# A two-layer transformer on one core: another opening with filler matmuls, and a landing price for transfers issued by ScalarE

## The chip, the core and the metric

The kernel runs on one core of one Trainium2 chip. The metric is the device time of one execution in microseconds; less is better. The engines are called PE (TensorE, the matmuls; PEld its weight loads), DVE (VectorE), ACT (ScalarE), POOL (GpSimd) and SP (SyncE, which here only issues transfers).

## The reference, cut to what matters

Two layers work on x of 256 tokens by 1024 channels, in float32. Each layer is a SwiGLU network, a mixer, and a second SwiGLU network, each behind a norm that is modulated by the condition c:

```python
c_act = jax.nn.silu(c)
for layer in range(2):
    mod = (c_act @ ada_w[layer] + ada_b[layer]).reshape(B, 3, 3, D_MODEL)
    h = modulate(x, norm_g[layer, 0], mod[:, 0, 0], mod[:, 0, 1])     # rmsnorm(x)*g*(1+scale)+shift
    x = x + 0.5 * mod[:, 0, 2][:, None, :] * swiglu(h, ffn_w13[layer, 0], ffn_w2[layer, 0])
    h = modulate(x, norm_g[layer, 1], mod[:, 1, 0], mod[:, 1, 1])
    y = swa_mixer(...) if layer == 0 else fox_mixer(...)
    x = x + mod[:, 1, 2][:, None, :] * y
    h = modulate(x, norm_g[layer, 2], mod[:, 2, 0], mod[:, 2, 1])
    x = x + 0.5 * mod[:, 2, 2][:, None, :] * swiglu(h, ffn_w13[layer, 1], ffn_w2[layer, 1])
# fox_mixer: log_f = log_sigmoid(fl + b_f); F = cumsum(log_f); s = q.k + F[q] - F[k], causal softmax, @ v
```

swa_mixer is attention in a window of 128 with a sink and a relative bias; both mixers have 16 query heads of 64 channels, and q and k are normed per head. The inner width of the SwiGLU networks is 2816. ada_w, the modulation's weights, is 1024 by 9216 in each layer.

## The kernel before

**Matmuls.** Every float32 product is three matmuls (`mm3`). `split` has ACT cast a landed weight piece `wraw` (128x1024, 512 KB) to `whi`, and DVE subtract to get the rest `wlo`; the activations are split in the same way into a high and a low part of hT. The three are whi by hT high, whi by hT low, and wlo by hT high. In the trace and in the order below all of them read `pa<-whi,hT` or `ps<-wlo,hT`; pa and ps are both PSUM banks.

**Order.** The whole program is first recorded, with every instruction on a named engine (or, through `rec.also`, on one of two). `Recorder.run` then plays a list scheduler over it: it gives each instruction a duration, works out due times from PE's order, and on each engine picks the ready instruction with the earliest due time; `rec.urgent` sets a due time by hand. A transfer's end is taken from its bytes at 400 GB/s behind the transfers before it, with 2000 ns more for those that POOL issues. The order in which the plan starts them is the order in which each engine's queue holds them on the chip, so an instruction whose input is late holds up all that stand behind it. Weights are issued by SP, at most 8 in flight. Since one helper emits everything, all instructions stand on one line (L238) in the profile, and tiles tell them apart.

**Opening.** SP loads c into one row of `gate`, then x in two halves, then the weights. ACT issues two small transfers (`colb`, the modulation's bias by column, and `gcol`, the norm gains); POOL issues `qkg` (gains of q and k), `sink` and `bfb` (the forget bias) through its software queue. ACT takes Silu of c (1x1024), two matmuls with `ones` broadcast it to 128 rows, and ACT copies it to `cb`. `rstd` squares x on ACT (t, ss, u, rs), `norm` scales it to `xn`, on DVE for the first half of the tokens and on ACT for the second. `start` transposes xn in 16 pieces into two tiles `xT`, of four k blocks each, and then runs the first 1024 of the inner columns in 8 k steps. A k step loads two pieces of ada, on which DVE makes two dot products with cb (`SCALAR_TENSOR_TENSOR wraw,mod<-wraw,cb`, written into `mod`), and two pieces of weight (`w13s`), and issues h, hT high (ACT), hT low (DVE) and 24 matmuls of 128x512.

**First FFN after that.** The other columns follow with `sil` (silu times up), its transposes (`ps<-ident,sil`) and `gT`, the high and low part of the transposed product, beside which DVE works off the rest of layer 0's modulation, paced by a table.

**Second mixer.** For groups of heads PE makes q and k, ACT squares them (`sq`), DVE sums (`qss`), POOL takes the power (`qrs`), DVE scales (`qn`), and PE transposes (`pa<-ident,qn`). `fox_maps` makes the running sums of log f, writes them to DRAM (`foxsc`) and reads them back to all partitions in four transfers of 512 KB, on ACT's queue, as `M`; DVE adds F and the mask (`M<-M,F,cmask`) before the softmax uses it (`t,nm<-ps,M`).

Of the kernel before, what the change touches and what calls it, by code (L numbers as in the profile page):

```python
# [44 lines left out]
TABLE = 1283.0  # L45
TC = {}
# [119 lines left out]
class Op:  # L166
    __slots__ = ("eng", "emit", "dur", "deps", "succ", "bases", "due", "n", "wait", "ready", "start", "end",
                 "bytes", "at", "bg", "urgent", "alts", "paced", "port", "part", "group", "table")
# [10 lines left out]
class Recorder:  # L179
    def __init__(self):  # L180
        self.ops, self.bases, self.slots, self.pe, self.releases = [], [], {}, 0.0, []
        self.bg, self.urgent, self.paced, self.marks, self.group = False, None, None, [], None

    def add(self, eng, real, method, a, k):
# [11 lines left out]
        o.table = None  # L196
# [95 lines left out]
    def run(self, window=None):  # L292
# [62 lines left out]
        pes = sorted((o for o in ops if o.eng == "PE"), key=lambda o: o.at)  # L355
        for o in ops:
            o.wait, o.ready = len(o.deps), 0.0
            if not o.wait:
                heapq.heappush(pending, (0.0, o.n))

        def finish(o, t, end):
# [12 lines left out]
            for s in o.succ:  # L374
                s.wait -= 1
                s.ready = max(s.ready, o.end + lat(o, s))
                if not s.wait:
                    heapq.heappush(pending, (s.ready, s.n))
                    heapq.heappush(events, s.ready)

        while len(done) < len(ops):
# [11 lines left out]
            for e in engines:  # L393
                while busy[e] <= t:
# [3 lines left out]
                    for i, (due, n) in enumerate(avail[e][:60]):  # L398
# [10 lines left out]
                        if fits(o):  # L409
# [13 lines left out]
                            break  # L423
                    if pick is None:
                        break
# [55 lines left out]
def _build(ctx, rec, tc, nc, ap, out):  # L481
# [23 lines left out]
    crow = gate[0:1]  # L505
    rec.urgent = -60e3
# [21 lines left out]
    ones = cp.tile([P, P], F32, name="ones")  # L528
    G.memset(ones, 1.0)
# [10 lines left out]
    qkg = cp.tile([P, 2, 2], F32, name="qkg")  # L540
    sink = cp.tile([P, NH], F32, name="sink")
    msink = cp.tile([P, NH], F32, name="msink")
    bfb = cp.tile([P, NH], F32, name="bfb")
# [134 lines left out]
    def norm(h, eng=None):  # L678
        rs = rstd(h)
        xn = []  # L680
        for dh in range(2):
            c = slice(dh * 512, dh * 512 + 512)
            t = bp.tile([P, 512], F32, tag="b", name="xn")
            if eng is A:
                A.activation(t, x[h][:, c], AF.Copy, scale=rs)
            else:
                V.tensor_scalar(out=t, in0=x[h][:, c], scalar1=rs, scalar2=None, op0=ALU.mult)
# [24 lines left out]
    def start(hT):  # L712

        xn = [norm(0), norm(1, A)]
        xT = []
        for g in range(2):
            t = wp.tile([P, 4, S], F32, tag="w", name="xT")
            for h in range(2):
                pt = psum()
                for j in range(4):  # L720
                    T.transpose(pt[:, j * P : j * P + P], xn[h][g][:, j * P : j * P + P], ident)
                A.copy(t[:, :, h * P : h * P + P], pt.rearrange("p (a b) -> p a b", a=4))
            xT.append(t)
        banks = [[pool_() for _ in range(2)] for pool_ in (pacc, pacc, psum, psum)]
        mod = new_mod()

        def modulated(k):
            for m in range(2):
# [3 lines left out]
            o = V.tensor_scalar(out=t, in0=xT[k // 4][:, k % 4, :], scalar1=mod[1][:, k : k + 1],  # L732
                                scalar2=mod[0][:, k : k + 1], op0=ALU.mult, op1=ALU.add)
            rec.also(o, A, "activation", t, xT[k // 4][:, k % 4, :], AF.Identity, scale=mod[1][:, k : k + 1],
                     bias=mod[0][:, k : k + 1])
# [5 lines left out]
        for k in range(KT):  # L741
# [3 lines left out]
            for c in range(NST):  # L745
                a = (c % 2) * 512
# [458 lines left out]
def _layout(inputs):  # L1205
# [28 lines left out]
    a["qkg"] = np.stack([np.stack([col(f["swa_q_g"][0]), col(f["swa_k_g"][0])], 1),  # L1234
                         np.stack([col(f["fox_q_g"][0]), col(f["fox_k_g"][0])], 1)], 1)
    a["sink"] = f["swa_sink"].reshape(1, NH)
    a["bf"] = f["fox_b_f"].reshape(1, NH)
# [28 lines left out]
```

## Time and profile before

| | |
|---|---|
| median of 3 runs | 995.08 us (993.34 to 995.79) |
| the profiled execution's own time | 994.5 us |
| its span in the trace | 992.7 us |
| granted TensorE clock, mean | 1.00 |
| busy: PE, DVE, ACT, POOL | 972.6, 776.9, 528.2, 48.2 us |
| moved by DMA | 252.73 MB, 255 GB/s over the span |

Times in the rows are microseconds from the span's start; a row of the timeline is the start, the busy time, the engine, the operation with output and inputs, a count, and in brackets the idle time before it with what ended it. A row of the waits is what waited, for what, and then the total, the number of times and the longest.

### The profile page before, as it was taken

What the parts mean: (1) busy time and instruction counts of PE and PEld (TensorE: products, weight loads), DVE (VectorE), ACT (ScalarE), POOL (GpSimd) and SP (SyncE); (2) the same over time, 40 slices, a digit from 0 to 9 for tenths busy, and PEclk for the clock granted to TensorE, in tenths of its full rate; (3) what the DMA queues carried; (4) which work ended last, traced back from release to release, by engine and by line L of the source; (5) the groups of instructions that cost most, each with busy time, mean ns of one, the idle gap of its engine ahead of it and who ended that gap; (6) DMA issues with size and microseconds to landing.
All of it is one profiled execution on the core that took longest, in us unless ns stands there. A gap on an engine that the chain in (4) does not pass through costs nothing.

```text
span 992.7 us, 13662 instructions
## 1 busy us (share of the span) xinstructions
PE 972.6 (98%) x4766; PEld 816.3 (82%) x4766; DVE 776.9 (78%) x1396; ACT 528.2 (53%) x946; POOL 48.2 (5%) x73
## 2 busy tenths in 40 slices
PE   6999999999999999999999999999999999999998
PEld 4878788798888888888888888889899888888886
DVE  5999989985899988767898788658788998554622
ACT  6583434465986454444554453437677776444420
POOL 1000000012100000000100000001221010000000
PEclk9999999999999999999999999999999999999999
DMA  9999999856347987776788879744437458656501
GB/s 338 409 390 383 402 361 409 307 172 215 129 156 252 337 334 285 291 294 233 275 317 304 312 279 352 247 157 161 139 112 266 161 197 282 224 198 220 211 8 64
DMA packets 74247, 252.73 MB, mean 255 GB/s; under 512 B 8497, under 2 KB 11969, under 8 KB 74178
## 3 DMA queue, kind: packets, MB, share of 16 engines
q1 hardware_dynamic: 73186, 249.63, 68.6%
q10 hardware_dynamic: 896, 2.21, 0.6%
q8 instruction: 37, 0.61, 0.2%
q0 software_dynamic: 96, 0.02, 0.2%
q14 instruction: 32, 0.26, 0.1%
HBM read 249.95 MB, written 1.88 MB: 254 GB/s over the span
## 4 chain that ended last, share of the span: by engine, by line
PE 91%; DVE 4%; ACT 2%; DMA 2%; issue 1%; POOL 0%; SPq 0%; DVEq 0%; POOLq 0%
PE ps L238 57%; PE pa L238 34%; DVE wraw L238 1%; DVE wlo L238 1%; DMA wraw<-in_w13s 1%; DMA M<-foxsc 1%; ACT t L238 1%; POOL qrs L238 0%; ACT PT L238 0%; DVE t L238 0%; DVE gT L238 0%; DVE sil L238 0%; ACT whi L238 0%; SPq L238 0%; DVE qss L238 0%
## 5 line engine op out<-in xcount | busy, mean ns | idle before, releaser
L238 PE MATMUL ps<-whi,hT 128*128 128x512 f32 (+2 forms) x1728 | 534.8, 382 | 0.0
L238 ACT CAST whi<-wraw 128x1024 fp32r<-128x1024 f32 (+2 forms) x328 | 329.5, 1024 | 218.6 <-DMA wraw<-in_w 72.4
L238 DVE TENSOR_TENSOR wlo<-wraw,whi 128x1024 fp32r<-128x1024 f32 (+2 forms) x328 | 381.3, 1180 | 67.0 <-ACT whi L238 49.2
L238 PEld LDWEIGHTS ps<-whi,hT 128*128 128x128 f32 x1728 | 321.5, 188 | 52.9 <-issue 0.6
L238 PE MATMUL ps<-wlo,hT 128*128 128x512 f32 (+2 forms) x864 | 328.1, 381 | 0.0
L238 PE MATMUL pa<-whi,gT 128*128 128x512 f32 x704 | 218.0, 391 | 0.0
L238 DVE SCALAR_TENSOR_TENSOR wraw<-wraw,cb 128x1024 f32<-128x1024 f32 x144 | 173.3, 1218 | 15.5 <-DMA wraw<-in_ada 15.1
L238 PEld LDWEIGHTS ps<-wlo,hT 128*128 128x128 f32 x864 | 162.4, 188 | 26.1 <-issue 0.2
L238 PEld LDWEIGHTS pa<-whi,gT 128*128 128x128 f32 x704 | 131.9, 188 | 27.2
L238 PE MATMUL pa<-wlo,gT 128*128 128x512 f32 x352 | 133.3, 390 | 0.0
L238 ACT ACTIVATE sil<-ps 128x256 f32<-128x256 f32 x84 | 32.0, 384 | 105.6 <-PE ps L238 105.4
L238 PEld LDWEIGHTS pa<-wlo,gT 128*128 128x128 f32 x352 | 66.1, 188 | 13.6
L238 DVE TENSOR_TENSOR sil<-sil,ps 128x256 f32<-128x256 f32 x84 | 34.6, 414 | 48.2 <-ACT sil L238 48.1
L238 DVE TENSOR_TENSOR gT<-ps,gT 128x256 fp32r<-128x256 f32 x88 | 33.5, 415 | 8.9 <-ACT gT L238 8.9
L238 PE MATMUL pa<-whi,OT 128*128 128x512 f32 x128 | 39.1, 393 | 0.0
L238 PE MATMUL pa<-PT,zeroed 128*128 128x256 f32 (+1 forms) x192 | 36.3, 287 | 0.5 <-DVE PT L238 0.4
L238 ACT ACTIVATE t<-x 128x512 f32<-128x512 f32 x24 | 15.0, 625 | 40.8 <-DVE x L238 38.9
L238 DVE SCALAR_TENSOR_TENSOR t<-gate,pa 128x512 f32<-128x512 f32 (+1 forms) x26 | 15.6, 640 | 25.6 <-DMA gate<-gsc 12.9
L238 ACT CAST gT<-ps 128x256 fp32r<-128x256 f32 x88 | 29.1, 378 | 12.2 <-PE ps L238 11.6
L238 PEld LDWEIGHTS pa<-PT,zeroed 128*128 128x128 f32 x192 | 30.1, 191 | 3.8 <-DVE PT L238 1.2
L238 POOL TENSOR_TENSOR qrs<-qss,mhalf 128x4 f32<-128x4 f32 (+1 forms) x24 | 26.8, 1118 | 87.3 <-DVE qss L238 86.3
L238 PE MATMUL ps<-ident,sil 128*128 128x128 f32 x176 | 27.9, 272 | 2.6 <-DVE sil L238 1.4
(113 smaller groups left out, 650.7 us busy)
## 6 DMA issues: line engine op xcount, KB each, us to landing
wraw<-in_ada SPq DMA_DIRECT2D x144, 512.0 KB, 7.5
wraw<-in_w13b SPq DMA_DIRECT2D x132, 512.0 KB, 6.3
wraw<-in_w SPq DMA_DIRECT2D x88, 512.0 KB, 5.6
wraw<-in_w13a SPq DMA_DIRECT2D x28, 512.0 KB, 10.2
wraw<-in_fwin SPq DMA_DIRECT2D x28, 384.0 KB, 3.8
wraw<-in_w13s SPq DMA_DIRECT2D x16, 512.0 KB, 10.2
wraw<-in_swin SPq DMA_DIRECT2D x16, 384.0 KB, 5.2
wraw<-in_swout SPq DMA_DIRECT2D x8, 512.0 KB, 3.7
```

The lines of the kernel that those rows point to most:

```text
L238: return lambda: getattr(real, method)(*[un(v) for v in a], **{n: un(v) for n, v in k.items()})
```

## The change

Two parts are made together. The opening: 21 filler matmuls of 128x512 on a tile of zeros (`wz`), which the scheduler issues on PE whenever nothing else is ready; the five small inputs in one transfer `small` on ACT's queue, none on POOL's; an early Silu of one column; the Silu of c in the evacuation of the broadcast; the squares of x on either of ACT and DVE; xn on DVE alone, piece by piece; the second half of the transposes inside k step 0; h always on ACT. And the plan's costs: a transfer over 100 KB that ACT issues lands 2400 ns later in the plan, which moves the order in the second mixer (`small` counts too).

```diff
+NWARM = 21
 # Recorder.run, the choice of the next instruction:
+                    if pick is None and e == "PE" and fillers and fillers[0].wait == 0 and t >= fillers[0].ready:
+                        o = fillers.pop(0)
+                        busy[e] = t + o.dur * (2 if cold else 1)
+                        active += busy[e] - t
+                        ...
+                        continue
 # Recorder.run, the cost of a DMA:
-                        o.end = dma + 2000 * (e == "POOL")
+                        o.end = dma + (2000 if e == "POOL" else 2400 if e == "ACT" and o.bytes > 1e5 else 0)
 # _build:
+    warm = psum()
+    wz = wp.tile([P, 512], F32R, tag="w", name="wz")
+    G.memset(wz.bitcast(F32), 0.0)
+    rec.filler = True
+    for _ in range(NWARM):
+        T.matmul(warm, wz[:, 0:P], wz, start=True, stop=True)
+    rec.filler = False
+    rec.urgent = -70e3
+    tb = cp.tile([P, 1], F32, name="tb")
+    A.activation(tb, ones[:, 0:1], AF.Silu)
...
-    colb = cp.tile([P, 2, 9, KT], F32, name="colb")
-    A.dma_start(colb, ap["colb"])
+    small = cp.tile([P, 232], F32, name="small")
+    A.dma_start(small, ap["small"])
+    colb = small[:, 0:144].rearrange("p (l s k) -> p l s k", l=2, s=9)
+    gcol = small[:, 144:192].rearrange("p (s k) -> p s k", s=6)
+    qkg = small[:, 192:196].rearrange("p (a b) -> p a b", a=2)
+    sink = small[:, 196:212]
+    bfb = small[:, 212:228]
-    gcol = cp.tile([P, 6, KT], F32, name="gcol")
-    A.dma_start(gcol, ap["gcol"])
...
-    A.activation(crow, crow, AF.Silu)
     for i in range(2):
         T.matmul(pc, ones[0:1, :], crow[:, i * 512 : i * 512 + 512], start=True, stop=True)
-        A.copy(cb[:, i * 512 : i * 512 + 512], pc)
+        A.activation(cb[:, i * 512 : i * 512 + 512], pc, AF.Silu)
...
-        G.dma_start(qkg, ap["qkg"])
-        G.dma_start(sink, ap["sink"].to_broadcast([P, NH]))
-        G.dma_start(bfb, ap["bf"].to_broadcast([P, NH]))
...
-    def rstd(h):
+    def rstd(h, first=False):
-            A.activation(t, x[h][:, c], AF.Square, scale=1.0 / 32.0, accum_out=ss[:, dh : dh + 1])
+            o = A.activation(t, x[h][:, c], AF.Square, scale=1.0 / 32.0, accum_out=ss[:, dh : dh + 1])
+            if first:
+                rec.also(o, V, "scalar_tensor_tensor", out=t, in0=x[h][:, c], scalar=1.0 / 1024.0, in1=x[h][:, c],
+                         op0=ALU.mult, op1=ALU.mult, accum_out=ss[:, dh : dh + 1])
...
     def start(hT):
-        xn = [norm(0), norm(1, A)]
+        rs = [rstd(h, True) for h in range(2)]
-        for g in range(2):
+        def transposed_x(g):
             for h in range(2):
+                xn = bp.tile([P, 512], F32, tag="b", name="xn")
+                V.tensor_scalar(out=xn, in0=x[h][:, g * 512 : g * 512 + 512], scalar1=rs[h], ...)
                 for j in range(4):
-                    T.transpose(pt[:, j * P : j * P + P], xn[h][g][:, j * P : j * P + P], ident)
+                    T.transpose(pt[:, j * P : j * P + P], xn[:, j * P : j * P + P], ident)
+        transposed_x(0)
...
-            o = V.tensor_scalar(out=t, in0=xT[k // 4][:, k % 4, :], scalar1=mod[1][:, k : k + 1], ...)
-            rec.also(o, A, "activation", t, xT[k // 4][:, k % 4, :], AF.Identity, ...)
+            A.activation(t, xT[k // 4][:, k % 4, :], AF.Identity, scale=mod[1][:, k : k + 1], bias=mod[0][:, k : k + 1])
...
             for c in range(NST):
+                if k == 0 and c == 1:
+                    transposed_x(1)
```

Lines are now L240. Nearly nothing changes in SP's queue; POOL loses its three transfers.

PE, from its first matmul, before (hT_214 is the high part, hT_226 the low part):

```order
L238 MATMUL ps<-gate,ones 128x512 x2
L238 MATMUL ps<-ident,xn 128x128 x16
L238 MATMUL pa<-whi,hT_214 128x512
L238 MATMUL pa<-wlo,hT_214 128x512
L238 MATMUL pa<-whi,hT_214 128x512
L238 MATMUL pa<-wlo,hT_214 128x512
L238 MATMUL pa<-whi,hT_214 128x512
L238 MATMUL pa<-whi,hT_226 128x512 x2
L238 MATMUL pa<-wlo,hT_214 128x512
```

and with the change (hT_209 and hT_220):

```order
L240 MATMUL ps<-wz 128x512 x4
L240 MATMUL ps<-gate,ones 128x512 x2
L240 MATMUL ps<-wz 128x512 x9
L240 MATMUL ps<-ident,xn 128x128 x4
L240 MATMUL ps<-wz 128x512 x2
L240 MATMUL ps<-ident,xn 128x128 x4
L240 MATMUL ps<-wz 128x512 x6
L240 MATMUL pa<-whi,hT_209 128x512
L240 MATMUL pa<-wlo,hT_209 128x512
L240 MATMUL pa<-whi,hT_209 128x512
L240 MATMUL pa<-wlo,hT_209 128x512
L240 MATMUL pa<-whi,hT_220 128x512 x2
L240 MATMUL ps<-ident,xn 128x128 x8
```

The fillers stand around the broadcasts and the transposes, and 8 transposes have moved behind the sixth real matmul.

ACT, from its first instruction, before:

```order
L238 DMA colb<-in_colb 128x144
L238 DMA gcol<-in_gcol 128x48
L238 ACT_TABLE_LOAD
L238 ACTIVATE gate<-gate 1x1024
L238 ACTIVATE t,ss<-x_94 128x512
L238 ACTIVATE t,ss<-x_99 128x512 x2
L238 COPY cb<-ps 128x512
L238 ACTIVATE t,ss<-x_94 128x512
L238 ACTIVATE xn<-x_99,rs 128x512
L238 COPY cb<-ps 128x512
L238 CAST whi<-wraw 128x1024
L238 COPY xT<-ps 128x4x128 x2
```

and with the change:

```order
L240 DMA small<-in_small 128x232
L240 ACT_TABLE_LOAD
L240 ACTIVATE tb<-ones 128x1
L240 ACTIVATE t,ss<-x_90 128x512
L240 ACTIVATE cb<-ps 128x512 x2
L240 COPY xT<-ps 128x4x128
L240 CAST whi<-wraw 128x1024
L240 COPY xT<-ps 128x4x128
L240 ACTIVATE h_207<-xT,mod_192,mod_178 128x256
L240 CAST hT_209<-h_207 128x256
```

Behind the weight's cast ACT now has one evacuation of xT ahead of h, where before it had two and an xn and a second cast.

In the k steps from 2 on, the low part of hT stands in DVE's queue behind two wlo instead of one.

DVE before the first gT of the first FFN, before:

```order
L238 TENSOR_TENSOR wlo<-wraw,whi 128x1024
L238 TENSOR_TENSOR sil<-sil,ps 128x256 x4
L238 TENSOR_TENSOR wlo<-wraw,whi 128x1024 x6
L238 TENSOR_TENSOR gT<-ps,gT 128x2x128 x8
L238 TENSOR_TENSOR sil<-sil,ps 128x256
L238 SCALAR_TENSOR_TENSOR wraw,mod_772<-wraw,cb 128x1024
```

and with the change:

```order
L240 TENSOR_TENSOR wlo<-wraw,whi 128x1024
L240 TENSOR_TENSOR sil<-sil,ps 128x256 x4
L240 TENSOR_TENSOR wlo<-wraw,whi 128x1024 x5
L240 TENSOR_TENSOR gT<-ps,gT 128x2x128 x8
L240 TENSOR_TENSOR sil<-sil,ps 128x256
L240 TENSOR_TENSOR wlo<-wraw,whi 128x1024 x2
```

One wlo of six has moved behind the gT.

DVE in the second mixer, at the first tile M, before:

```order
L238 TENSOR_TENSOR qn<-ps,qrs 128x256
L238 TENSOR_TENSOR wlo<-wraw,whi 128x768
L238 SCALAR_TENSOR_TENSOR M_6799<-M_6799,F,cmask 128x256
L238 SCALAR_TENSOR_TENSOR M_6856<-M_6799,F,cmask 128x128
L238 TENSOR_REDUCE qss<-sq 128x4
L238 TENSOR_SCALAR qss<-qss 128x4
L238 SCALAR_TENSOR_TENSOR M_6799<-M_6799,F,cmask 128x256
L238 TENSOR_TENSOR zeroed<-ps,zeroed 128x2x64
L238 TENSOR_TENSOR qn<-ps,qrs 128x256
L238 SCALAR_TENSOR_TENSOR M_6856<-M_6799,F,cmask 128x128
L238 SCALAR_TENSOR_TENSOR M_6799<-M_6799,F,cmask 128x256
```

and with the change:

```order
L240 TENSOR_TENSOR qn<-ps,qrs 128x256
L240 TENSOR_TENSOR wlo<-wraw,whi 128x768
L240 TENSOR_REDUCE qss<-sq 128x4
L240 TENSOR_SCALAR qss<-qss 128x4
L240 TENSOR_TENSOR zeroed<-ps,zeroed 128x2x64
L240 TENSOR_TENSOR qn<-ps,qrs 128x256
L240 SCALAR_TENSOR_TENSOR M_6816<-M_6816,F,cmask 128x256
L240 SCALAR_TENSOR_TENSOR M_6908<-M_6816,F,cmask 128x128
```

qss and qn stand ahead of the work on M, where before two instructions on M stood ahead of qss and a third behind it.

More of the change, by code (lines that the diff above doesn't have):

```diff
@@ L167 @@
     __slots__ = ("eng", "emit", "dur", "deps", "succ", "bases", "due", "n", "wait", "ready", "start", "end",
-                 "bytes", "at", "bg", "urgent", "alts", "paced", "port", "part", "group", "table")
+                 "bytes", "at", "bg", "urgent", "alts", "paced", "port", "part", "group", "table", "filler")
 class Engine:
@@ L354, in run @@
         low, group, last, table = 0, None, None, None
-        pes = sorted((o for o in ops if o.eng == "PE"), key=lambda o: o.at)
+        pes = sorted((o for o in ops if o.eng == "PE" and not o.filler), key=lambda o: o.at)
+        fillers = [o for o in ops if o.filler]
         for o in ops:
             o.wait, o.ready = len(o.deps), 0.0
-            if not o.wait:
+            if not o.wait and not o.filler:
                 heapq.heappush(pending, (0.0, o.n))
@@ L376, in finish @@
                 s.ready = max(s.ready, o.end + lat(o, s))
-                if not s.wait:
+                if not s.wait and not s.filler:
                     heapq.heappush(pending, (s.ready, s.n))
@@ L505, in _build @@
     crow = gate[0:1]
+    ones = cp.tile([P, P], F32, name="ones")
+    G.memset(ones, 1.0)
+    warm = psum()
[8 more added lines that the diff above has]
+    A.activation(tb, ones[:, 0:1], AF.Silu)
     rec.urgent = -60e3
@@ L676, in rstd, with norm @@
         return rs
-    def norm(h, eng=None):
+    def norm(h):
         rs = rstd(h)
```

27 lines of the change are left out of this document (10 added, 17 removed).

## The prediction

> **What bounds the kernel now.** I read the page first: busy times, then the chain that ended last.
>
> ```profile
> PE 972.6 (98%) x4766; PEld 816.3 (82%) x4766; DVE 776.9 (78%) x1396; ACT 528.2 (53%) x946; POOL 48.2 (5%) x73
> PE 91%; DVE 4%; ACT 2%; DMA 2%; issue 1%; POOL 0%; SPq 0%; DVEq 0%; POOLq 0%
> ```
>
> PE (TensorE) is busy for 98% of the span of 992.7 us and carries 91% of the chain. Nothing but PE's holes, and slow matmuls, can be won. So the second view is what PE waited for, added up by releaser:
>
> ```profile
> PE ps L238 <- ACT xn L238: 5.1, 2, 3.2
> PE ps L238 <- ACT gate L238: 4.1, 1, 4.1
> PE ps L238 <- DVE gT L238: 2.1, 2, 1.2
> PE pa L238 <- DVE qn L238: 1.5, 2, 1.2
> PE ps L238 <- DVE sil L238: 1.4, 1, 1.4
> ```
>
> 9.2 us of the 15 us or so lie in the opening (gate, xn), 3.5 in the first FFN (gT, sil), 1.5 at qn, in the two mixers. The third view is the chain, in order of time, over the first 27 us; columns are start, length, what:
>
> ```profile
> 2.96 9.41 DMA wraw<-in_w13s
> 12.40 1.05 ACT whi L238
> 13.82 0.59 ACT xT L238
> 14.41 0.63 ACT xn L238
> 15.09 1.97 PE ps L238 x8
> 17.06 4.54 PE pa L238 x12
> 21.59 2.74 PE ps L238 x12
> ```
>
> The opening is bound by the landing of the first weight tile at 12.37 (2.96 + 9.41), its cast, and the second half of the transposes, which ACT's queue had delayed. The first 12 real matmuls took 4.54 us, the next 2.74, so 1.8 us went to a slow start. The page's granted clock is 1.00 in this very stretch, so that column doesn't show the slowness; the durations do.
>
> Why the weight landed so late is in the table of one-microsecond windows (PE, PEld, DVE, ACT, POOL busy, then granted clock, DMA share, GB/s), and in the queues of the first 12 us (packets, MB, share of the 16 engines):
>
> ```profile
> 5.00:6.00 1.00, 1.00 (x3) 0.36 (x2) 0.00 (x0) 0.60 (x2) 0.00 (x0) 1.00 1.05 289
> 6.00:7.00 1.00, 1.00 (x3) 0.30 (x1) 0.17 (x1) 0.40 (x1) 0.00 (x0) 1.00 1.48 295
> 7.00:8.00 1.00, 0.87 (x2) 0.00 (x0) 0.03 (x1) 1.00 (x5) 0.00 (x0) 1.00 0.77 30
> 8.00:9.00 1.00, 0.00 (x0) 0.00 (x0) 0.19 (x1) 1.00 (x4) 0.57 (x1) 1.00 0.69 247
> 20.00:70.00 50.00, 49.38 (x224) 40.79 (x223) 48.85 (x77) 34.73 (x52) 0.00 (x0) 1.00 1.03 405
> 70.00:80.00 10.00, 9.40 (x42) 7.72 (x43) 10.00 (x20) 5.62 (x9) 0.00 (x0) 1.00 0.89 324
> q0 software_dynamic: 96, 0.02, 13.5%
> q10 hardware_dynamic: 288, 0.10, 3.3%
> ```
>
> From 5 to 9 us, 289 + 295 + 30 + 247 = 861 KB moved where 4 us at 405 GB/s carry 1620: a hole of 759 KB, or 1.9 us. In it stand the 96 packets of the software queue (qkg, sink, bfb): 13.5% of 16 engines over 12 us is 25.9 us, 0.27 us a packet and 1.6 us an engine, for 0.02 MB. ACT's own queue (q10: colb, gcol) took 22 ns a packet.
>
> **The opening, step by step.**
>
> *The software-queue transfers go.* Their bytes come in `small`, 119 KB on ACT's queue, which replaces 96 KB of colb and gcol there: 0.3 us of wire at 405 GB/s between, less the 18 KB of the three. If the hole is theirs, the first weight lands 1.9 us earlier, at 10.5. Bounds: 0 (the hole has another cause) and 1.9. I take 1.9, since their 1.6 us an engine nearly fills it. The Trainium skill (DMA: Bandwidth & Descriptors, Bandwidth) puts the floor of a small transfer at about 10.5 ns per packet. By that price 96 packets would be 1 us of one engine, an estimate, and taking them away would move nothing; the trace's 0.27 us a packet decides against it here.
>
> *The path to the first real matmul.* ACT's order is now the first xT evacuation, whi, the second xT, h, hT; the squares of x (three of four) and all xn are on DVE, and gate's Silu (1x1024, 1.05 us ahead of the broadcasts) is folded into the two evacuations. On the path after the landing stand whi, xT, h and hT:
>
> ```profile
> 12.40 1.05 ACT L238 CAST whi<-wraw 128x1024 fp32r<-128x1024 f32 x1 [2.28 <-DMA wraw<-in_w13s]
> 15.86 0.60 ACT L238 ACTIVATE h<-xT,mod,mod 128x256 f32<-128x256 f32 x1
> 16.50 0.40 ACT L238 CAST hT<-h 128x256 fp32r<-128x256 f32 x1
> 16.95 0.80 PE L238 MATMUL pa<-whi,hT 128*128 128x512 f32 x1
> 10.59 1.22 DVE L238 SCALAR_TENSOR_TENSOR wraw<-wraw,cb 128x1024 f32<-128x1024 f32 x1
> ```
>
> 10.5 + 1.05 + 0.59 (xT, from the chain) + 0.60 + 0.40 gives 13.1, less about 0.2 of overlap between neighbours on ACT: 12.9 instead of 16.95, 4.0 earlier. The dots don't end last: from cb at about 7 to 8.5 us, two of 1.22 end near 11. The three squares and two xn added to DVE fall before the first dot, where DVE stood idle. The table load moves ahead of the landing of c and costs nothing, hidden by that DMA.
>
> *The fillers.* 21 of them of 0.2 to 0.4 us run where PE waited anyway (9.2 us above). Each is issued only when nothing else is ready in the plan, so one can hold up a real instruction by its own length, 0.4 us at most; the path runs over the weight's landing, so I cost them at nothing. If they keep PE active until 12.9, the 1.8 us of slow start are won. Bounds 0 and 1.8; I take 1.8, since in the trace 4.5 us of matmuls were enough to end the slowness and 21 fillers are more than that. The Trainium skill (TensorE: Matmul & The Clock Gate, Part 4) says that transposes don't count as activity for the clock. By that rule the stretch of the first 8 transposes, and of the waits around them, counts as idle, which speaks for the lower bound if the fillers behind them end early; no run here shows it yet.
>
> *Eight transposes move into k = 0*, behind the first 6 matmuls. 13 warm ones took 1.58 us, so eight take 1.0 on PE's path:
>
> ```profile
> 67.80 1.58 PE L238 MATMUL ps<-ident,sil 128*128 128x128 f32 x13
> ```
>
> *The low half of hT comes one wlo later on DVE* from k = 2 on. wlo is 1.15 us (6.89 over six, below); DVE is busy 48.85 of the 50 us to 70, so there is little to absorb it, but it can cost only once, since DVE's work per k step stays the same. Bounds 0 and 1.2; I take the middle, 0.6.
>
> PE's lead at 20 us: 4.0 + 1.8 - 1.0 - 0.6 = 4.2 (bounds 2.3, without the 1.9, and 4.8).
>
> **How much of it lives to 190 us.** In the first FFN PE waits at 69, 109 and 187 us for DVE, whose work is fed by the DMA stream (405 GB/s and a share of 1.03 from 20 to 70 us, above):
>
> ```profile
> 63.31 6.89 DVE L238 TENSOR_TENSOR wlo<-wraw,whi 128x1024 fp32r<-128x1024 f32 x6
> 70.59 0.44 PE L238 MATMUL ps<-ident,sil 128*128 128x128 f32 x2 [1.21 <-DVE gT L238]
> 109.54 0.27 PE L238 MATMUL ps<-ident,mod 128*8 128x128 f32 x1 [0.89 <-DVE gT L238]
> 133.63 1.23 DVE L238 SCALAR_TENSOR_TENSOR wraw<-wraw,cb 128x1024 f32<-128x1024 f32 x1 [1.71 <-DMA wraw<-in_ada]
> 188.13 0.44 PE L238 MATMUL ps<-ident,sil 128*128 128x128 f32 x2 [1.39 <-DVE sil L238]
> ```
>
> Of PE's 4.2 only what DVE and DMA can follow survives. DMA leads by 1.9; the dip at 70 to 80 us (324 GB/s for 405, 2.0 us of stream) came from buffers that DVE and PE freed late, and an earlier PE may fill some of it. Besides, five wlo instead of six now stand ahead of gT at 69, which is worth 1.15 there. So the lead at 190 is at least 1.9 + 1.15 = 3.0 if the feed decides, and 4.2 if PE's lead passes whole. I take 3.7, a little above the middle, as the dip's share comes on top of the lower end. After 190 PE hardly waits until the second mixer, so the lead stays.
>
> **The second mixer.** M is read back on ACT's queue, and the new price of 2.4 us moves DVE's work on M behind the qss and qn that PE waits for.
>
> ```profile
> 702.01 5.80 DMA M<-foxsc
> 706.34 0.38 ACT L238 ACTIVATE sq<-ps 128x256 f32<-128x256 f32 x1 [2.94 <-PE ps L238]
> 707.83 0.94 DVE L238 SCALAR_TENSOR_TENSOR M<-M,F,cmask 128x256 f32<-128x256 f32 x2 [1.79 <-DMA M<-foxsc]
> 708.69 0.41 DVE L238 TENSOR_REDUCE qss<-sq 128x4 f32<-128x256 f32 x1
> 709.44 1.11 POOL L238 TENSOR_TENSOR qrs<-qss,mhalf 128x4 f32<-128x4 f32 x1 [4.73 <-DVE qss L238]
> 710.59 0.42 DVE L238 TENSOR_TENSOR qn<-ps,qrs 128x256 f32<-128x256 f32 x1 [0.70 <-POOL qrs L238]
> 711.07 0.44 PE L238 MATMUL pa<-ident,qn 128*128 128x128 f32 x2 [1.23 <-DVE qn L238]
> ```
>
> DVE sat 1.79 us at the head of its queue for M, with qss behind it, whose input sq was there at 706.72. Put first, qss starts about 1.95 us earlier, qn ends at 711.01 - 1.95 = 709.1, and PE comes to its transposes at 711.07 - 1.23 = 709.84: the stall of 1.23 goes, with 0.7 to spare. M, landed at 707.80, is then worked at about 709.1, late by 1.2; its first user was DVE's own row softmax at 711.58. The order around the other M loads shifts as well; bounds for the rest are a gain of 0.3 (the other wait for qn, 1.5 in all less 1.23) and a loss of one more stall of 1.23. I take 0 for the rest, and 1.2 here.
>
> **Sum.** 3.7 + 1.2 = 4.9 against the profiled execution's own 994.5 (span 992.7): 989.6. The median of the three runs is 0.6 above that execution, so 990.2 us. 0.3%, about what a measurement of this kernel can tell from no change, is 3.0 us.
>
> **Rivals.**
> - *The hole is not the software queue's*, or `small`, 128 rows of 928 bytes, makes one of its own. For it: the hole stands where the stream turns from x to the weights, with ACT's queue beside it, and that queue stays. Against: the DMA share is 1.48 and 0.77 in the hole, so engines were held by packets that carried almost nothing. The first matmul would come at 14.9, PE's lead be 2.3, and the feed would let 1.15 pass; with 1.2 in the mixer 995.1 - 2.4 = 992.7. Chance 0.14. This is also how it would come out by the Trainium skill's price per packet (DMA: Bandwidth & Descriptors, Bandwidth).
> - *The feed binds to 187 us, and the moved wlo only comes back later* (DVE 10.00 of 10.00 at 70 to 80). Then 1.9 + 1.2 = 3.1: 992.0. Chance 0.16.
> - *DVE's waits at 109 and 187 go as well*, since sil and gT are ahead of wlo there too: 0.89 + 1.39 on top, with part of it hindered by the feed, 987.5. Chance 0.12.
> - *Slower: the qn stall spreads.* In the new order the work on M and the row softmax of one group stand ahead of the next group's qss, as M did at 707.83; each of the 16 qn groups can then stall PE by 1.23. Against the opening's 3.7, it needs six of 16 to be over 0.3% slower: 995.1 - 3.7 + 7.4 = 998.8. Against it: ahead of qss now stands work whose data has landed, not a wait for DMA. Chance 0.06.
>
> The forecast has 0.52. Faster by over 0.3% (below 992.1): 0.52, 0.12 and half of the second rival, 0.72; within 0.3%: the first and the other half, 0.22; slower 0.06. The range goes from 986.8 (lead 4.8, the two DVE waits gone, 1.2 in the mixer, and the 0.6) to 994.2, which holds the first rival with a mixer that gives nothing.
>
> **What would show it.** The first `pa<-whi,hT` at 12.9 with 0.23 us spacing at once (fillers); DMA over 380 GB/s in each microsecond from 5 to 9 (software queue); PE's wait for gT near 66 under 0.5; no 1.79 wait for M, and no PE wait for qn near 705. The forecast fails if the weights still land at 12.4, if the first twelve matmuls take 4.5, or if PE's waits for DVE in the first FFN grow by what the opening won.

## The result, and the profile after

The changed kernel took 989.61 us (median of six runs, 989.23 to 992.39), the kernel before 995.24 (six runs, 993.31 to 996.18): a ratio of 0.995, 95% interval 0.994 to 0.996. Predicted were 990.2 us, with 986.8 to 994.2 as the range. The profiled execution took 989.23 with a span of 987.5, which is 5.2 less than the 992.7 before. The total came out close; the parts of the sum did not, as the sections below show.

The page's busy times, and PE's waits by releaser, of the changed kernel:

```profile
PE 978.3 (99%) x4787; PEld 821.1 (83%) x4787; DVE 779.3 (79%) x1405; ACT 524.2 (53%) x937; POOL 46.6 (5%) x71
PE ps L240 <- POOL wz L240: 1.5, 1, 1.5
PE pa L240 <- ACT hT L240: 0.9, 1, 0.9
PE pa L240 <- DVE t L240: 0.4, 1, 0.4
PE ps L240 <- DVE gT L240: 0.4, 1, 0.4
PE ps L240 <- DVE sil L240: 0.3, 1, 0.3
PE pa L240 <- DVE qn L240: 0.2, 1, 0.2
```

The 9.2 us of waits for gate and xn are gone, but PE's busy time has risen by 5.7: the fillers are counted as busy. In the first network the waits for gT and sil fell from 3.5 to 0.7, the wait for qn from 1.5 to 0.2.

The DMA stream from 5 to 9 us (columns as in the prediction), and the DVE rows ahead of the first gT:

```profile
5.00:6.00 1.00, 1.00 (x2) 0.33 (x1) 0.89 (x5) 1.00 (x3) 0.01 (x1) 1.00 0.98 393
6.00:7.00 1.00, 1.00 (x2) 0.00 (x0) 0.93 (x5) 0.17 (x1) 0.54 (x1) 1.00 0.98 401
7.00:8.00 1.00, 1.00 (x3) 0.73 (x3) 0.96 (x4) 0.60 (x1) 0.21 (x1) 1.00 1.03 422
8.00:9.00 1.00, 1.00 (x3) 0.76 (x3) 0.55 (x3) 0.00 (x0) 0.52 (x1) 1.00 1.03 422
60.77 5.76 DVE L240 TENSOR_TENSOR wlo<-wraw,whi 128x1024 fp32r<-128x1024 f32 x5
66.45 2.74 DVE L240 TENSOR_TENSOR gT<-ps,gT 128x256 fp32r<-128x256 f32 x8
```

The hole is filled: 393 GB/s or more in each microsecond, where it was 30 in the worst. The chain over the opening shows that this isn't what the first matmul now waits for:

```profile
1.46 10.07 PE ps L240 x21
11.55 0.59 ACT xT L240
12.14 0.34 ACT whi L240
12.99 0.59 ACT xT L240
13.61 0.61 ACT h L240
14.24 0.41 ACT hT L240
14.70 1.65 PE pa L240 x6
16.35 0.87 PE ps L240 x8
17.22 1.39 PE pa L240 x6
18.61 2.74 PE ps L240 x12
```

No transfer stands in it. From 1.46 to 11.53 it is PE itself, fillers, broadcasts and transposes, then ACT. The first real matmul starts at 14.70, not at the predicted 12.9; the first twelve took 1.65 + 1.39 = 3.04 us instead of 4.54.

The clock column of the windows can't show that: a trace has no clock record ahead of its first one at full clock, and the column counts the time before it as 1.00. That first record begins at 10.4 to 13.1 us in the six profiles with fillers (10.6 in this one), and at 14.8 to 20.5 in the five without (20.5 in the kernel before). So the fillers do bring the full rate forward; e3 below, which lacks only them, has 17.2.

To see where each microsecond came from, take the start of one and the same matmul in both traces and subtract (the median over 3 us at each place): PE's lead over the profile before. The first column is the start of the first real matmul; the others stand at times of the kernel before: 60 us (first network), 205 (behind it), 262 and 284 (within and behind the tail of the first mixer), 757 and 790 (ahead of and behind the tail of the second), 985.

| kernel | first matmul | 60 | 205 | 262 | 284 | 757 | 790 | 985 |
|---|---|---|---|---|---|---|---|---|
| before | 16.95 | 0 | 0 | 0 | 0 | 0 | 0 | 0 |
| changed | 14.70 | 2.89 | 6.00 | 5.92 | 4.67 | 6.21 | 4.90 | 4.83 |
| changed, another profile (e9) | 15.42 | 2.19 | 4.89 | 4.80 | 4.79 | 6.32 | 4.99 | 4.93 |
| e1 opening only | 15.08 | 2.54 | 4.96 | 4.92 | 3.64 | 3.82 | 3.81 | 3.78 |
| e2 mixer only | 16.59 | 0.63 | 0.63 | 0.61 | -0.44 | 0.96 | -0.33 | -0.36 |
| e3 no fillers | 13.90 | 2.19 | 5.09 | 5.07 | -1.75 | -0.11 | -1.42 | -1.35 |
| e4 software queue back | 15.42 | 2.23 | 5.61 | 5.54 | 5.54 | 7.16 | 5.83 | 5.85 |
| e5 late fillers | 13.76 | 3.84 | 6.43 | 6.34 | 5.25 | 6.77 | 5.47 | 5.43 |
| e6 early gT | 16.52 | 0.39 | 1.81 | 1.83 | -5.96 | -5.73 | -5.75 | -5.75 |
| e7 merge only | 15.22 | 3.12 | 2.26 | 2.21 | 2.21 | 2.90 | 2.88 | 2.85 |
| e8 late fillers, M behind | 13.28 | 4.32 | 7.43 | 7.35 | 6.32 | 7.07 | 7.08 | 7.04 |

The same opening gave 2.19, 2.54 and 2.89 at 60 us in three profiles (and e2, whose opening is the one before, 0.63), so a difference of 0.7 in that column between single profiles says nothing.

One thing must be read out of the way first. Between 262 and 284 the changed kernel lost 1.25 us though no wait grew. The windows there (columns as before) show why; the second fence has e3 in the same stretch, the third the second profile of the changed kernel:

```profile
260.00:265.00 5.00, 4.96 (x36) 4.13 (x35) 4.61 (x20) 4.92 (x20) 0.00 (x0) 1.00 0.31 103
265.00:270.00 5.00, 5.00 (x28) 4.60 (x28) 2.90 (x18) 2.84 (x11) 0.00 (x0) 0.66 0.01 3
```

```profile
260.00:275.00 15.00, 15.00 (x63) 13.21 (x63) 8.87 (x41) 8.45 (x30) 0.00 (x0) 0.50 0.12 37
```

```profile
260.00:275.00 15.00, 14.69 (x107) 12.54 (x107) 13.26 (x56) 13.97 (x48) 0.00 (x0) 1.00 0.21 70
```

The granted clock fell to half there, in the softmax part of the first mixer, for 3.4 us in the changed kernel's profile and 17 us in e3's (63 matmuls in 15 us where 107 ran at full clock). Runs differ in it, so a median over few runs carries it: runs whose mean clock is 0.989 to 0.991 are some 3 to 10 us above the median of the others of the same kernel.

### The profile page after: what moved, and what is told of

Same layout as the page of the kernel before. It is cut to its first block, busy times and chain, and to the rows that moved or that the text cites. A ratio compares the mean times of both kernels' runs of the same rounds, so it can differ in the third digit from the quotient of the medians.

```text
span 987.5 us, 13699 instructions
## 1 busy us (share of the span) xinstructions
PE 978.3 (99%) x4787; PEld 821.1 (83%) x4787; DVE 779.3 (79%) x1405; ACT 524.2 (53%) x937; POOL 46.6 (5%) x71
## 3 DMA queue, kind: packets, MB, share of 16 engines
q10 hardware_dynamic: 752, 2.23, 0.6%
## 4 chain that ended last, share of the span: by engine, by line
PE 93%; DVE 4%; ACT 1%; issue 1%; POOL 1%; DVEq 0%; POOLq 0%
PE ps L240 59%; PE pa L240 34%; DVE wlo L240 1%; DVE wraw L240 1%; POOL qrs L240 1%; DVE M L240 0%; DVE t L240 0%; DVE qss L240 0%; ACT whi L240 0%; DVE PT L240 0%; ACT t L240 0%; DVE qn L240 0%; ACT sil L240 0%; ACT PT L240 0%; DVE sil L240 0%
## 5 line engine op out<-in xcount | busy, mean ns | idle before, releaser
L240 PE MATMUL ps<-whi,hT 128*128 128x512 f32 (+2 forms) x1728 | 534.6, 382 | 0.0
L240 ACT CAST whi<-wraw 128x1024 fp32r<-128x1024 f32 (+2 forms) x328 | 328.7, 1024 | 211.8 <-DMA wraw<-in_w 73.0
L240 DVE TENSOR_TENSOR wlo<-wraw,whi 128x1024 fp32r<-128x1024 f32 (+2 forms) x328 | 381.2, 1182 | 61.4 <-ACT whi L240 48.0
L240 PEld LDWEIGHTS ps<-whi,hT 128*128 128x128 f32 x1728 | 321.5, 188 | 52.9 <-DVE wraw L240 0.6
L240 PE MATMUL ps<-wlo,hT 128*128 128x512 f32 (+2 forms) x864 | 328.0, 381 | 0.0
L240 PE MATMUL pa<-whi,gT 128*128 128x512 f32 x704 | 218.0, 391 | 0.0
L240 DVE SCALAR_TENSOR_TENSOR wraw<-wraw,cb 128x1024 f32<-128x1024 f32 x144 | 173.4, 1219 | 15.8 <-DMA wraw<-in_ada 15.5
L240 PEld LDWEIGHTS ps<-wlo,hT 128*128 128x128 f32 x864 | 162.4, 188 | 26.1 <-issue 0.2
L240 PEld LDWEIGHTS pa<-whi,gT 128*128 128x128 f32 x704 | 131.8, 188 | 27.1
L240 PE MATMUL pa<-wlo,gT 128*128 128x512 f32 x352 | 133.0, 390 | 0.0
L240 ACT ACTIVATE sil<-ps 128x256 f32<-128x256 f32 x84 | 32.1, 385 | 104.2 <-PE ps L240 104.1
L240 PEld LDWEIGHTS pa<-wlo,gT 128*128 128x128 f32 x352 | 66.1, 188 | 13.7
L240 DVE TENSOR_TENSOR sil<-sil,ps 128x256 f32<-128x256 f32 x84 | 34.8, 416 | 50.4 <-ACT sil L240 50.2
L240 DVE TENSOR_TENSOR gT<-ps,gT 128x256 fp32r<-128x256 f32 x88 | 33.6, 417 | 9.6 <-ACT gT L240 9.4
L240 PE MATMUL pa<-whi,OT 128*128 128x512 f32 x128 | 38.7, 391 | 0.0
L240 PE MATMUL pa<-PT,zeroed 128*128 128x256 f32 (+1 forms) x192 | 37.4, 296 | 0.9 <-DVE PT L240 0.6
L240 ACT CAST gT<-ps 128x256 fp32r<-128x256 f32 x88 | 29.0, 377 | 11.3 <-PE ps L240 10.8
L240 DVE SCALAR_TENSOR_TENSOR t<-gate,pa 128x512 f32<-128x512 f32 (+1 forms) x26 | 15.6, 642 | 23.9 <-DMA gate<-gsc 13.1
L240 PEld LDWEIGHTS pa<-PT,zeroed 128*128 128x128 f32 x192 | 30.7, 199 | 4.3 <-DVE PT L240 1.4
L240 ACT ACTIVATE t<-x 128x512 f32<-128x512 f32 x21 | 13.1, 626 | 38.5 <-DVE x L240 36.3
L240 POOL TENSOR_TENSOR qrs<-qss,mhalf 128x4 f32<-128x4 f32 (+1 forms) x24 | 26.3, 1094 | 87.2 <-DVE qss L240 87.1
L240 ACT ACTIVATE t<-t,nm 128x129 f32<-128x129 f32 (+3 forms) x64 | 28.9, 454 | 2.1 <-DVE nm L240 1.9
```

The source lines that it names most:

```text
L240: return lambda: getattr(real, method)(*[un(v) for v in a], **{n: un(v) for n, v in k.items()})
```

## The experiments

**e1, the opening alone.** The changed kernel without the landing price for the mixer's loads:

```diff
-o.end = dma + (2000 if e == "POOL" else 2400 if e == "ACT" and o.bytes > 1e5 else 0)
+o.end = dma + (2000 if e == "POOL" else 2400 if e == "ACT" and 1e5 < o.bytes < 2e5 else 0)
```

> The changed kernel with the landing price of 2400 ns kept for the small transfer alone, so that the opening has the new order and the second mixer the old one. Theory A (the mixer's new order gains 1.2 to 1.5 us at the first qn and gives it back in the tail of the same mixer): the time is that of the changed kernel within 0.5 us, about 989.8; PE's wait of 1.2 us for qn near 704 is back, and the tail near 760 to 780 loses about 1.3 us less than in the changed kernel. Theory B (the prediction: 1.2 us of the gain is the mixer's): 1.2 us more than the changed kernel, about 990.8.

989.76 us, ratio 0.9949 (0.9937 to 0.9961): the changed kernel's gain without the mixer's new order. PE's wait for qn is back (start, busy time, and the wait in brackets):

```profile
707.32 0.44 PE L240 MATMUL pa<-ident,qn 128*128 128x128 f32 x2 [1.18 <-DVE qn L240]
```

In the table its lead stays from 690 to 985 us (3.67 to 3.78), while the changed kernel's rises to 6.21 and falls to 4.90. From 284 to 985 us the two gain the same, 0.14 here and 0.16 there. Theory A holds.

**e2, the mixer alone.** The kernel before with the new price:

```diff
-o.end = dma + 2000 * (e == "POOL")
+o.end = dma + (2000 if e == "POOL" else 2400 if e == "ACT" and o.bytes > 1e5 else 0)
```

> The kernel before with nothing but the landing price of 2400 ns in the plan's costs; only the second mixer's order changes. Theory A (given back in the tail): 995 within 0.5 us of the kernel before, though the wait of 1.23 us for qn near 710 is gone. Theory B (prediction): 1.2 us less than before, about 994.0.

994.35 us, ratio 1.0001 (0.9991 to 1.001): nothing. From 284 to 757 us it gains 1.40, by 790 it has lost 1.29 of it. New waits stand in the tail, in this kernel and, at the same instructions, in the changed one:

```profile
766.88 0.38 PE L238 MATMUL pa<-PT,zeroed 128*128 128x256 f32 x1 [0.24 <-ACT PT L238]
770.75 0.30 PE L238 MATMUL pa<-ident,t 128*128 128x128 f32 x1 [0.46 <-DVE t L238]
775.96 0.95 PE L238 MATMUL pa<-PT,zeroed 128*128 128x256 f32 x6 [0.21 <-DVE PT L238]
```

With two of 0.08 and 0.14 they sum to 1.13, where the kernel before had 0.28 + 0.39 = 0.67 there; the other 0.8 of the loss is in no single wait, and was not followed further. Theory A holds: from 284 to 985 us the lead gains 0.08 here, 0.16 in the changed kernel, and 0.14 in e1, which has the old order, so the new order is worth nothing that these profiles can tell.

**e3, no fillers.**

```diff
-NWARM = 21
+NWARM = 0
```

> The changed kernel with no filler matmul (NWARM = 0). Theory A (the fillers, 0.43 us each, hold up the transposes by about 2 us and so the weight's cast behind them on ACT, but spare the slow start): the first real matmul at about 12.5 instead of 14.70, its first twelve slow (about 4.5 us with the 8 transposes beside), so k step 1 begins within 0.7 us of the changed kernel's 21.35, and the time is within 0.7 us. Theory B (the prediction: fillers cost nothing and win 1.8): first matmul at 14.7 still, k step 1 about 1.8 later, 1.8 us slower in the end.

995.56 us, ratio 0.9991 (0.9974 to 1.0007), which looks like a loss of 6 us by itself. It isn't the opening's: 8 of the 12 runs have a mean clock of 0.989 to 0.991 and took 993.88 to 996.99; the other four took 989.72 to 991.13. In the profile the lead is 5.07 at 262 us, within the changed kernel's 4.80 to 5.92, and -1.75 at 284, all of it in the stretch at half clock shown above. The opening's chain:

```profile
3.03 8.19 DMA wraw<-in_w13s
11.25 1.04 ACT whi L240
13.90 2.93 PE pa L240 x6
17.93 1.37 PE pa L240 x6
19.30 2.72 PE ps L240 x12
```

Without fillers the first matmul comes at 13.90, bound by the weight again (it and the second half of x landed 1.1 to 1.3 later in this run than in the changed kernel's profile), but its first six take 2.93 instead of 1.65, and k step 1 starts at 22.02 against 21.35. So the fillers spare 1.3 us of slow start and cost 0.8 of delay here; with the changed kernel's landings the delay would be nearer 1.9, an estimate from the 0.8 and the 1.1. The lead at 60 us is 2.19, where the same opening with fillers has 2.19 to 2.89: as they were placed, the 21 fillers won 0.7 us at most. Theory A, as far as the opening goes; the run times can't tell more. Why so many runs of this kernel lost the clock in the first mixer, whose instructions are the changed kernel's in the same order, stays open.

**e4, the software queue back.** The changed kernel with three transfers on POOL again:

```diff
+        G.dma_start(qkg, ap["qkg"])
+        G.dma_start(sink, ap["sink"].to_broadcast([P, NH]))
+        G.dma_start(bfb, ap["bf"].to_broadcast([P, NH]))
```

> The changed kernel with the three transfers qkg, sink and bfb back on POOL's software queue, as before; everything else of the opening stays. Theory A (they make the hole in the DMA stream): a microsecond with under 100 GB/s between 5 and 9 us is back, the first weight lands 1.9 to 2.3 later than 10.07, near 12.2; the first real matmul only moves by what the fillers no longer hide, 0.5 to 1.5 us; the feed is later by 2 us, and the time by 1 to 2.5 us, about 991 to 992. Theory B (the hole has another cause): the weight lands at 10.1 and the time stays within 0.3 us.

988.76 us, ratio 0.995 (0.9932 to 0.9968). The hole is back, in the stream's rows and in the queue (packets, MB, share over the first 12 us):

```profile
6.00:7.00 1.00, 1.00 (x2) 0.00 (x0) 0.81 (x3) 0.35 (x1) 0.57 (x1) 1.00 1.53 337
7.00:8.00 1.00, 1.00 (x3) 0.73 (x3) 0.96 (x6) 0.60 (x1) 0.00 (x0) 1.00 0.91 87
8.00:9.00 1.00, 1.00 (x3) 0.76 (x3) 0.56 (x3) 0.00 (x0) 0.72 (x1) 1.00 0.59 186
q0 software_dynamic: 96, 0.02, 12.1%
```

The first weight landed at 11.70 instead of 10.07. So theory A is right on the cause and wrong on the price: the time is no longer, the lead at 205 us is 5.61. The landing also scatters by itself: 11.70 to 12.37 in the four profiles with the software queue, 10.05 to 11.99 in the seven without, the latest of these in e9, where the second half of x landed at 8.15 instead of 6.12. The weight was not what the first matmul waited for, and the feed was not what the first network waited for. PE stood behind the fillers:

```profile
7.17 4.21 PE L240 MATMUL ps<-wz 128*128 128x512 f32 x9
11.18 1.05 PE L240 MATMUL ps<-ident,xn 128*128 128x128 f32 x4
15.42 0.50 PE L240 MATMUL pa<-whi,hT 128*128 128x512 f32 x1 [0.72 <-ACT hT L240]
```

**e5, late fillers.** 14 instead of 21; the last six only once the 2 broadcasts and 8 transposes have been issued in the plan:

```diff
-NWARM = 21
+NWARM = 14
+NLATE = 6
-if pick is None and e == "PE" and fillers and fillers[0].wait == 0 and ...
+if pick is None and e == "PE" and fillers and (len(fillers) > NLATE or low >= 10) and fillers[0].wait == 0 and ...
```

> The changed kernel with 14 fillers instead of 21, of which the last 6 may only come when the first 8 transposes have been issued; every other queue is as in the changed kernel. Theory A (nine fillers of 0.43 us ahead of the transposes hold them up by about 2 us, and ACT's cast of the first weight behind them): transposes begin near 9.0 instead of 10.92, the first real matmul comes at 12.7 to 13.3 instead of 14.70; if the clock is up by then, k step 1 begins at 19.6 to 20.2 instead of 21.35, PE's lead over the kernel before at 60 us is 3.9 to 4.6 instead of 2.5 to 2.9, and the time near 988. If it is slow at the start, at most 1.8 of that is lost again. Theory B (the prediction: the weight's landing decides, fillers cost nothing): first matmul at 14.7, no change.

988.59 us, ratio 0.995 (0.9926 to 0.9974), with four of twelve runs at a mean clock of 0.989 to 0.991 (993.05 to 996.79); the other eight took 986.37 to 990.39. The timeline of PE:

```profile
7.17 2.08 PE L241 MATMUL ps<-wz 128*128 128x512 f32 x4
9.21 1.68 PE L241 MATMUL ps<-ident,xn 128*128 128x128 f32 x8
10.64 1.63 PE L241 MATMUL ps<-wz 128*128 128x512 f32 x6
13.76 0.50 PE L241 MATMUL pa<-whi,hT 128*128 128x512 f32 x1 [1.49 <-ACT hT L241]
14.10 0.39 PE L241 MATMUL pa<-wlo,hT 128*128 128x512 f32 x1
```

The transposes begin at 9.21 instead of 10.92, the first matmul at 13.76, with x and the first weight landing 1 us later in this run than in the changed kernel's profile (11.01 for 10.07), and the matmuls are fast at once. K step 1 starts at 20.39 (21.35), and the lead at 60 us is 3.84. Theory A, 0.5 us short of it at the first matmul; the chain of this opening goes back to the landing of x at 7.17 (6.12 in the changed kernel's profile).

**e6, an early gT.** The kernel before, where the plan makes DVE's gT and sil of the first network due 2500 ns earlier (`early` holds these instructions):

```diff
-            o.due = due
+            o.due = due - (2500 if o in early else 0)
```

> The kernel before with the due times of DVE's sil and gT products of the first network 2500 ns earlier in the plan, so that five wlo instead of six stand ahead of the first gT and the later ones move likewise; opening, transfers and mixers as before. Theory A (the order of DVE's queue, not a later feed, made PE wait at 69, 109 and 187 us): PE's 3.5 us of waits there fall to under 1, PE's lead at 205 us is 2.5 to 3, the time 2 to 3 us less than before. Theory B (the prediction: the feed of DVE and DMA decides): waits return elsewhere in the first network, lead at 205 us at most 1.2.

992.32 us, ratio 0.9994 (0.9968 to 1.0021); the interval is wide because five of twelve runs lost the clock (999.02 to 1001.61), and the profile with them, 7.8 us between 262 and 284. The other seven took 990.82 to 992.40, which is 2.5 to 4.1 below the 994.88 of the kernel before. Ahead of that place the profile speaks for itself:

```profile
PE ps L239 <- DVE sil L239: 1.6, 2, 1.4
PE ps L239 <- DVE gT L239: 0.4, 1, 0.4
```

The waits for gT fell from 2.1 to 0.4, those for sil stayed (1.4, now 1.6), and the lead grew from 0.39 to 1.81 between 60 and 205 us. Half of theory A: the order of DVE's queue alone, with opening and feed as before, takes 1.5 of the 3.5 us of waits away. It does so in the steps of the changed kernel: the lead rises by 0.81 at 70 us and by 1.04 at 109, there by 0.80 and 1.04. The third step is missing: near 187 us the lead falls by 0.4 here, and rises by 1.1 in the changed kernel (0.5 to 1.5 in the other profiles of its plan). Ahead of that sil DVE has four dot products (1.15 us each) in the kernel before and three in the changed one, which is also an order, but no run makes this move alone, so that step is argued and not shown.

**e7, one transfer alone.** The kernel before with the five small inputs in `small` and none on POOL's queue:

```diff
-    A.dma_start(colb, ap["colb"])
-    A.dma_start(gcol, ap["gcol"])
-        G.dma_start(qkg, ap["qkg"])
-        G.dma_start(sink, ap["sink"].to_broadcast([P, NH]))
-        G.dma_start(bfb, ap["bf"].to_broadcast([P, NH]))
+    A.dma_start(small, ap["small"])
```

> The kernel before with its five small inputs in one transfer on ACT's queue and nothing on POOL's; the opening otherwise as before. Theory A (the hole in the stream is the software queue's, but what the first matmul waits for is mostly the second half of the transposes behind ACT's queue): no microsecond under 240 GB/s from 5 to 9 us, first weight near 10.3 instead of 12.37, first real matmul 0.5 to 2 us earlier than 16.95, time 0.5 to 2 us less than before. Theory B (the prediction's 1.9 passes whole): first matmul 1.9 to 2.3 earlier, 2 us less than before.

993.04 us, ratio 0.9975 (0.9958 to 0.9993). No microsecond from 5 to 9 us is under 377 GB/s, and the first weight landed at 10.23. The first matmul came at 15.22, 1.73 earlier, and it was fast, without any filler:

```profile
10.42 2.82 PE L238 MATMUL ps<-ident,xn 128*128 128x128 f32 x12 [3.02 <-ACT xn L238]
13.41 1.11 PE L238 MATMUL ps<-ident,xn 128*128 128x128 f32 x4 [0.17 <-DVE xn L238]
15.22 0.50 PE L238 MATMUL pa<-whi,hT 128*128 128x512 f32 x1 [0.69 <-ACT hT L238]
15.56 0.40 PE L238 MATMUL pa<-wlo,hT 128*128 128x512 f32 x1
```

From 10.42 on PE had run nothing but these 16 transposes, and the trace's full-clock record begins at 14.8, ahead of the first real matmul.

The lead of 3.12 at 60 us was 4.48 at 180 (this plan, too, has fewer waits for gT: 0.9 for 2.1), and 2.26 at 205. Of that fall 0.65 is a longer wait for sil, and 1.55 the clock, which went to half right behind it:

```profile
184.30 0.44 PE L238 MATMUL ps<-ident,sil 128*128 128x128 f32 x2 [2.04 <-DVE sil L238]
185.00:190.00 5.00, 5.00 (x16) 3.94 (x16) 5.00 (x10) 3.35 (x6) 0.00 (x0) 0.66 0.90 349
```

By the medians this one part is worth 1.8 us (993.04 for 994.88). In the profile the lead at 985 us is 2.85; without the fall of the clock it would be about 4.4, an estimate from the 1.55. Neither theory had that fall.

**e8, late fillers and one move in the second mixer.** The opening of e5, the mixer's old order, and the first instructions on M behind the next qn (only that move is shown; the fillers are those of e5, and the price is kept for `small` alone, as in e1):

```diff
+        part = done[a : z + 1]          # from the first M<-M,F,cmask to the next qn, in the plan's order
+        done[a : z + 1] = [o for o in part if o not in mset] + [o for o in part if o in mset]
```

> The opening of the late fillers (14, six of them behind the first transposes), and the second mixer in its old order but for one move: DVE's three instructions on the first tile M stand behind the next qss and qn instead of ahead of them. Theory A (the first qn's wait is worth 1.2 us, and what the changed kernel gave back in the tail of that mixer came from the order of the rest, not from that move): PE waits under 0.2 us for qn near 702, the tail loses nothing against the kernel before, PE's lead at the end is 1.2 to 1.6 us over the same kernel with the old mixer, so 1 us under the late fillers alone: 986 to 987 where the granted clock holds. Theory B (the tail is bound by DVE and ACT whatever stands ahead, so any lead won at the first qn is given back there): the tail loses 1.2 us, the time is that of the late fillers, 987 to 988.6.

987.21 us (985.85 to 988.43), ratio 0.9923 (0.9909 to 0.9936), the lowest median of all, and faster than the changed kernel, whose second set of runs, e9, stands beside it on the same chip (988.42 to 989.92). What the move in the mixer adds to the late fillers is read from the lead and not from the times: the eight runs of e5 above a mean clock of 0.991 have a median of 987.55. The first matmul came at 13.28. Between 690 and 985 us the lead rises from 6.36 to 7.04 and nothing of it is given back in the tail. It is 0.7, not 1.2 to 1.6; a good part of the rest is that another qn waits now:

```profile
714.21 0.44 PE L242 MATMUL pa<-ident,qn 128*128 128x128 f32 x2 [0.42 <-DVE qn L242]
```

Theory A, with its size halved: the loss in the tail belonged to the rest of the new order.

**e9, the changed kernel again.**

> The changed kernel, unaltered, on the same chip as the best version. All theories: 989 to 990 where the granted clock holds, PE's lead over the kernel before 2.5 to 2.9 at 60 us, 5 to 6 at 205 us; the tail of the second mixer gives back 1.3. If the granted clock falls to 0.5 in the tail of the first mixer at random, some of the runs are 6 to 8 us slower, and the profile may show it.

989.12 us (988.42 to 989.92), ratio 0.9942 (0.9929 to 0.9954). Its profile kept the clock in the first mixer and so shows the change without that: lead 4.80 at 262 us, 4.79 at 284. Its opening was slower, as the table says: x and the first weight landed 2 us later, and the first four transposes and the two fillers behind them ran at the slow rate (1.06 and 1.20 us for 0.60 and 0.71).

## Why the prediction was right, and where it was not

The time was right within 0.6 us, but by luck: three terms were too high, one was much too low, and one loss was not in the sum at all.

- *The software queue makes the hole.* Right as to the hole: e4 brings it back, e7 takes it away alone. The 1.9 us are less sure. This pair of profiles has 2.3 (12.37 to 10.07), but over all eleven the first weight lands at 12.0 on average with the software queue and at 10.7 without, 1.3 apart. The Trainium skill's 10.5 ns per packet (DMA: Bandwidth & Descriptors, Bandwidth) doesn't describe these 96 packets; e4's took 0.24 us each (12.1% of 16 engines over 12 us).
- *The path to the first real matmul, 4.0 us.* Too high; it was 2.25 (16.95 to 14.70). The step that failed is "I cost them at nothing", of the fillers. I named 0.4 us as what a filler can hold up, but the plan had nine of them in a row ahead of the first transposes, and at the slow rate they held PE from 7.17 to 10.92. xn stood ready at 9.04 (8.55 + 0.49). ACT's cast of the weight waits behind the first xT and so behind PE. Where the fillers are moved (e5, e8) the first matmul comes at 13.76 and 13.28. The changed kernel's rows:

```profile
8.55 0.49 DVE L240 TENSOR_SCALAR xn<-x,rs 128x512 f32<-128x512 f32 x1 [0.45 <-POOL rs L240]
7.17 3.91 PE L240 MATMUL ps<-wz 128*128 128x512 f32 x9
10.92 0.60 PE L240 MATMUL ps<-ident,xn 128*128 128x128 f32 x4
```

- *The slow start, 1.8.* 1.5 was won in this profile. e3 shows 1.3 for the first six matmuls; but e7's first matmuls were fast with no filler, and in the three profiles of the change's opening (the changed kernel, e1, e9) the full clock came at 10.6, 11.4 and 13.1 us, over 9 us after the first filler at 1.46. That transposes count for nothing, which the prediction set beside this term, is not borne out: in e7 PE ran 16 transposes and nothing else from 10.42 on, and the full clock came at 14.8. The Trainium skill (TensorE: Matmul & The Clock Gate, Part 1) says that the gate watches a window that runs freely and doesn't reset with the kernel, so that the moment varies from run to run; the three moments, 2.5 us apart, do vary.
- *Eight transposes in k = 0, 1.0.* 0.87. *hT's low part, 0.6.* At most 0.1: the twelve matmuls of k step 2 took 2.80 for 2.72.
- *How much lives to 190 us, 3.7 of 4.2.* Wrong in its mechanism. I let the feed limit the lead; instead the lead grew, from 2.2 to 2.9 at 60 us to 4.9 to 6.0 at 205, as PE's waits for DVE went, 3.5 to 0.7. e4 kept that growth with a feed 1.6 us later. e6 shows the first two of its three steps, 0.8 of them the place of gT behind five wlo instead of six (forecast as 1.15), as the order's alone; the third, near 187 us, is argued. This was the third rival, at 0.12, with an opening worth less than forecast; that rival's own sum should read 990.2 - 0.89 - 1.39 = 987.9, and not 987.5.
- *The second mixer, 1.2.* The wait went as described, and 1.5 us were there at 757 (e1, with the old order, has 0.2 of them); the step that failed is "I take 0 for the rest". The rest lost 1.3 in the tail. I had bounded it by a single stall of 1.23 and then left it out.
- *Not in the sum:* the granted clock in the first mixer, 1.25 us in this profile.

Put together from the profile: 2.89 at 60 us, + 3.11 to 205, - 0.08, - 1.25 for the clock, + 1.54 up to 757, - 1.31 in the tail and - 0.07 is the 4.83 at 985; the end of the span adds 0.4, which makes 5.2. Forecast were 4.2 - 0.5 + 1.2 = 4.9. That these agree is luck: the opening brought 1.3 less than forecast, the first network 3.6 more, the second mixer 1.0 less, and the clock took 1.25. The slower rival (qn stalls in many groups) did not come: one wait for qn of 0.2 us in all is left in the page's list.

## What to carry to other kernels

A filler is free only where nothing real can be ready: put it behind the last instruction that feeds another engine, and price it at the slow rate, since it runs before the clock is up. When a change moves a planner's order, follow the lead of one engine through both traces to the end of the stage, as a wait that is gone at its head may be paid back at its tail. And look at the granted clock by stage before explaining a difference between medians.

## What was not expected of the hardware

The granted clock fell to 0.5 in the first mixer's attention in seven of eleven profiles, for 3.4 us (changed kernel, e1, e2, e5, e8) or for 17 to 20 us (e3, e6), and in e7 for 3.4 us behind a wait of PE of 2.04 us at 184; in no other stage between the opening and the last 3 us. It lasted about 3.4 us or a multiple: 3.4 from 266.6 in the changed kernel, 17.1 from 259.5 in e3. In all eleven traces every change of the clock lies a whole multiple of 3.413 us after the first full-clock record, 75 and 76 of them in the changed kernel, 71 and 76 in e3. The Trainium skill (TensorE: Matmul & The Clock Gate, Why this matters for your kernels) warns of idle gaps over about 3 us; here 2.04 was followed by the drop, and in the kernel before 1.39 was not. In the changed kernel PE was busy for 4.96 of the 5 us ahead of the row with the drop, so a nearly full busy column doesn't keep the clock; the work there is 128-column scores, transposes (`pa<-ident,t`) and products. The Trainium skill (TensorE: Matmul & The Clock Gate, Part 4) says that matmuls in transpose mode don't count as PE-busy in the same way, which would point at this place. Whether this kernel's transposes run in that mode no trace shows, and two things speak against it as the cause: in e7 transposes alone stood ahead of the rise to the full clock, and the 3.4 us ahead of the drop (263.2 to 266.6) hold three transposes, where the three stretches of that length before it hold four to six. What drops the clock in the mixer stays open.
